# Layer 0's feed-forward: context up projections first, main tokens with 7 of 8 block products, gated products through DRAM, three down passes

## The chip, the cores and the metric

The kernel runs on one core of a Trainium2 chip, as one program in one launch. A core has a matrix engine (TensorE; PE in the profile, PEld its weight loads), VectorE (DVE), ScalarE (ACT), GpSimd (POOL) and SyncE (SP), which here only issues DMAs. The metric is the device time of one execution in microseconds (us); lower is better.

## The reference, cut to what matters

A two-layer transformer over 1024 main tokens and 256 context tokens of width 1024: layer 0 mixes with window and differential attention, layer 1 with gated linear attention (GLA). Each layer ends with a feed-forward of width 2816 with a convolution of 3 tokens. Layer 0 runs it on main and context tokens, layer 1 on main tokens alone. All values are float32.

```python
def conv_ffn(x, w_up, conv_w, conv_b, w_down):
    h = x @ w_up                       # [n, 1024] x [1024, 5632]
    h = lax.conv_general_dilated(h, ...) + conv_b      # each column: tokens t-1, t, t+1
    u, gt = jnp.split(h, 2, axis=-1)
    return (jax.nn.silu(gt) * u) @ w_down              # [n, 2816] x [2816, 1024]

for layer in range(2):
    ...
    h = h + g1 * y
    h = h + g2 * conv_ffn(rms_norm(h, norm2_g[layer]) * (1.0 + sc2) + sh2, ...)
    if need_ctx:                                       # layer 0
        hc = hc + cg1 * yc
        hc = hc + cg2 * conv_ffn(rms_norm(hc, norm2_g[layer]) * (1.0 + csc2) + csh2, ...)
```

## The kernel before

**Numbers.** Every operand of a large matmul is split into a high and a low part of a shorter float format (`split`, line 97: ACT casts the high part at L100, DVE subtracts to get the low part at L80). A product is three matmuls: high x high, high x low, low x high.

**Layout.** Features lie on the 128 partitions, tokens along the free axis. `h[k]` (k = 0 to 7) holds the residual stream, 1280 tokens: main blocks MAIN0 and MAIN1 of 512, then CTX of 256.

**Weights.** `load_w` (line 103) loads one block of 1024 x 128 weights (512 KB) with one DMA from SP into one of two raw buffers (`wraw`), and splits it in two halves of 512 columns into four of the twelve `wf` buffers (names `wh`, `wl`), so that the weights of three blocks can stand ready. A raw buffer is free again after DVE's second subtraction.

**Layer 0's feed-forward** (`ffn`, line 898) goes through 22 blocks c of 128 hidden features. For each, two up blocks (u and gate) are multiplied with all 1280 tokens into three PSUM banks (`big`, `proj` L130: 8 k x 3 matmuls for MAIN0, CTX and MAIN1), ACT and DVE apply the convolution (`cv`), ACT the silu, DVE the product, and the result is split into `gh`, `gl` in SBUF. After every second c, `down` (L923) multiplies the waiting pair with its two blocks of `ffn_down`, 8 output blocks d for each of CTX, MAIN0, MAIN1, and DVE adds each result to `h` (L77). The steps of layer 1's modulation (`mod_steps`: 32 blocks of 512 KB into `mraw`, two buffers, each reduced by DVE at L290) are laid between, two for each c. The norms ahead (`norm_mod`) and those of layer 1 behind (`norm3`) sum their squares first.

**Layer 1's feed-forward** is written in another way. `ffn_halves` (line 1060) splits the 1024 main tokens in two halves, the 1024 inputs in two halves, and pairs the u and gate blocks of a c; the 2 x 2 x 2 products of such blocks are made with seven products of sums and differences instead of eight (`forms_first`, `forms_last` build the token operands B11, B21, B22, T1 to T4 from `h`, whose memory then serves as workspace; `pair_forms` builds the weight operands). The gated products go to DRAM (`gs`, POOL's queue). `down_pass` (line 1157) runs once for each 512 tokens: eight PSUM banks collect over all 22 blocks, each with its weights loaded anew and its `gs` rows loaded into `dx` and split into `dh`, `dl`.

**What sets the order.** The Tile scheduler fixes the order of each engine's instructions when the program is built; engines run their lists in order and wait on semaphores. Inside `manual_schedule` PE's list follows the program text. In layer 0 that holds from the second half of the attention output to the first up blocks; in layer 1 from the output projection to the end. SP issues its DMAs in list order, and a DMA whose buffer is not free holds up those behind it.

## Time and profile before

| | us |
|---|---|
| median of 3 runs (3154.15 to 3158.14) | 3154.94 |
| the profiled execution | 3159.17 |
| its span, first to last instruction | 3157.4 |
| PE busy in it | 2999.3 (95%) |
| layer 0's feed-forward, start of its first up and of its last down matmul | 914.3 to 1864.0 |
| layer 1's feed-forward, start of its first block product and of its last down matmul | 2451.6 to 3140.4 |

A row of a view shows start and duration in us. A matmul's duration includes its flow through the array, so that neighbours overlap: what a matmul costs in a row of them is the distance between two starts. In a row of groups the first number after the bar is busy time, the second the mean of one instruction in ns. A bracket at the end of a row of the timeline is the time that the engine sat idle before it, and what ended that.

### The profile page before, as it was taken

The page shows a single profiled execution, that of the slowest core. Times are in us where ns is not written, and L with a number is a line of the kernel's source. Part 1 is how long each engine was busy: PE and PEld are TensorE (multiplying, and loading weights), DVE is VectorE, ACT ScalarE, POOL GpSimd, SP SyncE. Part 2 cuts the span into 40 slices and gives each one's busy share as a digit, 9 for nine tenths or more (in the row PEclk, how much of TensorE's full clock was granted, in tenths as well). Part 3 has the DMA queues.
Part 4 walks back from the last instruction along what each step waited for, and adds up shares of the span by engine and source line. Part 5 has one row for each costly group of instructions (what it writes and reads, how often), then busy time and mean ns, then how long its engine had stood idle before and what let it go on. Part 6 is the DMA issues. An engine that isn't in the chain of part 4 may idle for free.

```text
span 3157.4 us, 40797 instructions
## 1 busy us (share of the span) xinstructions
PE 2999.3 (95%) x16024; PEld 2523.0 (80%) x16024; DVE 2140.0 (68%) x3520; ACT 1290.8 (41%) x2301; POOL 50.5 (2%) x88
## 2 busy tenths in 40 slices
PE   8887789999999999999999999999999799999998
PEld 4676779998877888888888878888887588888886
DVE  7667578887478645555554498687686888887354
ACT  5111167777352222222222265454454444445332
POOL 0000000000000000000000000000001000000000
PEclk9988889999999999999999999999999999999999
DMA  6665582121525311111111132111134222225452
GB/s 218 180 177 164 154 203 67 55 61 34 174 81 164 110 34 41 41 34 41 35 38 36 38 131 74 51 36 42 51 112 157 66 88 80 81 80 166 151 169 95
DMA packets 154296, 300.50 MB, mean 95 GB/s; under 512 B 24468, under 2 KB 81940, under 8 KB 154104
## 3 DMA queue, kind: packets, MB, share of 16 engines
q1 hardware_dynamic: 133400, 261.94, 26.0%
q0 software_dynamic: 19552, 33.87, 3.8%
q8 instruction: 126, 2.06, 0.3%
q10 hardware_dynamic: 1152, 2.10, 0.2%
q14 instruction: 66, 0.54, 0.1%
HBM read 246.69 MB, written 51.12 MB: 94 GB/s over the span
## 4 chain that ended last, share of the span: by engine, by line
PE 77%; DVE 12%; DMA 6%; ACT 3%; issue 1%; SPq 0%; DVEq 0%; ACTq 0%
PE big L130 31%; PE bk L1090 13%; PE sm L923 9%; PE bk L1175 7%; DMA mraw<-in_mod_wt_dram 5%; PE sm L534 2%; PE sm L583 2%; PE sm L649 2%; PE big L509 2%; PE big L468 2%; PE sm L1610 2%; PE big L517 2%; DVE mraw L290 1%; PE sm L1541 1%; DVE junk L290 1%
## 5 line engine op out<-in xcount | busy, mean ns | idle before, releaser
L100 ACT CAST wh<-wraw 128x512 fp32r<-128x512 f32 x436 | 268.4, 621 | 897.8 <-PE big L130 444.6
L80 DVE TENSOR_TENSOR wl<-wraw,wh 128x512 fp32r<-128x512 f32 x436 | 299.6, 689 | 421.8 <-ACT wh L100 402.0
L130 PE MATMUL big<-x2h,wh 128*128 128x512 f32 (+1 forms) x1056 | 377.9, 358 | 2.4 <-ACT x2h L83 1.3
L130 PE MATMUL big<-x2l,wh 128*128 128x512 f32 (+1 forms) x1056 | 377.7, 358 | 0.4 <-DVE x2l L77 0.3
L130 PE MATMUL big<-x2h,wl 128*128 128x512 f32 (+1 forms) x1056 | 377.4, 357 | 0.0
L77 DVE SCALAR_TENSOR_TENSOR h<-sm,G,h 128x512 f32<-128x512 f32 (+1 forms) x280 | 180.8, 657 | 79.7 <-PE sm L923 78.8
L130 PEld LDWEIGHTS big<-x2h,wh 128*128 128x128 f32 x1056 | 199.1, 189 | 34.3 <-ACT crow L83 2.0
L130 PEld LDWEIGHTS big<-x2l,wh 128*128 128x128 f32 x1056 | 199.1, 189 | 32.5 <-DVE x2l L77 1.1
L130 PEld LDWEIGHTS big<-x2h,wl 128*128 128x128 f32 x1056 | 199.0, 188 | 30.4
L923 PE MATMUL sm<-gh,wh 128*128 128x512 f32 (+1 forms) x528 | 190.9, 361 | 6.3 <-DVE h L77 6.0
L923 PE MATMUL sm<-gl,wh 128*128 128x512 f32 (+1 forms) x528 | 188.6, 357 | 0.0
L923 PE MATMUL sm<-gh,wl 128*128 128x512 f32 (+1 forms) x528 | 187.9, 356 | 0.0
L77 DVE SCALAR_TENSOR_TENSOR cv<-big,cw,cv 128x255 f32<-128x255 f32 (+1 forms) x176 | 155.0, 881 | 31.8 <-ACT cv L83 29.6
L130 PE MATMUL big<-x1h,wh 128*128 128x512 f32 (+1 forms) x336 | 126.3, 379 | 33.8 <-DVE slo L80 32.7
L1175 PE MATMUL bk<-dh,wh 128*128 128x512 f32 x352 | 137.3, 390 | 0.0
L1175 PE MATMUL bk<-dl,wh 128*128 128x512 f32 x352 | 136.9, 389 | 0.0
L1175 PE MATMUL bk<-dh,wl 128*128 128x512 f32 x352 | 136.9, 389 | 0.0
L290 DVE CUSTOM_DVE_ANT_0 junk<-mraw,crow 128x1024 bf16<-128x1024 f32 x56 | 68.5, 1223 | 99.5 <-DMA mraw<-in_mod_wt_dram 99.5
L83 ACT ACTIVATE cv<-big,cb,cw 128x1024 f32<-128x1024 f32 x88 | 77.8, 884 | 135.7 <-DVE cv L77 134.5
L130 PE MATMUL big<-x1h,wl 128*128 128x512 f32 (+1 forms) x336 | 125.8, 375 | 3.9 <-DVE wl L80 3.9
L130 PE MATMUL big<-x1l,wh 128*128 128x512 f32 (+1 forms) x336 | 125.8, 375 | 0.0
L923 PEld LDWEIGHTS sm<-gh,wh 128*128 128x128 f32 x528 | 100.4, 190 | 29.6 <-DVE h L77 14.7
(442 smaller groups left out, 7491.0 us busy)
## 6 DMA issues: line engine op xcount, KB each, us to landing
mraw<-in_mod_wt_dram SPq DMA_DIRECT2D x88, 512.0 KB, 4.5
wraw<-in_ffn_up_dram SPq DMA_DIRECT2D x66, 512.0 KB, 3.7
wraw<-in_ffn_down_dram SPq DMA_DIRECT2D x66, 512.0 KB, 3.7
graw<-in_ffn_up_dram SPq DMA_DIRECT2D x22, 512.0 KB, 3.7
gs<-hh POOLq DMA_DIRECT2D x22, 512.0 KB, 2.9
dx<-gs SPq DMA_DIRECT2D x44, 256.0 KB, 3.8
q<-qs SPq DMA_DIRECT2D x40, 256.0 KB, 3.3
q<-qs SPq DMA_DIRECT2D x80, 128.0 KB, 3.5
```

What stands on the lines that cost most here:

```text
L77: return self.nc.vector.scalar_tensor_tensor(out=out, in0=in0, scalar=scalar, in1=in1, op0=op0, op1=op1)
L80: return self.nc.vector.tensor_tensor(out=out, in0=a, in1=b, op=op)
L83: return self.nc.scalar.activation(out=out, in_=in_, func=func, **kw)
L100: self.nc.scalar.copy(hi, src)
L130: self.nc.tensor.matmul(ps[:, t0:t0 + n], self.columns(a, k * m, m), b(k, t0, n), start=(k == 0 and j == 0), stop=(k == KD - 1 and j == 2))
L290: self.nc.vector.tensor_tensor_reduce(out=out, in0=raw, in1=row, scale=1.0, scalar=0.0, op0=ALU.mult, op1=ALU.add, accum_out=dst[:, v:v + 1])
L468: self.nc.tensor.matmul(ps[:, 256 * b:256 * b + 256], a(k, t0, P), self.columns(w, k % 4 * 256, 256), start=(k == 0 and j == 0), stop=(k = ...
L509: nc.tensor.matmul(out, q[:, 0, s, :], key, start=True, stop=False)
L517: nc.tensor.matmul(out, q[:, 1, s, :], key, start=False, stop=True)
L923: nc.tensor.matmul(o, self.columns(w, d * P, P), x[:, t0:t0 + n], start=(i == 0), stop=(i == 3 * len(group) - 1))
L1090: nc.tensor.matmul(ps, a[:, s], b, start=(start and k == 0 and j == 0), stop=(k == 3 and j == 2), skip_group_check=True)
L1175: nc.tensor.matmul(ps[d], self.columns(a, d * P, P), b, start=(c == 0 and j == 0), stop=(c == NFF - 1 and j == 2))
```

## The change

Layer 0's feed-forward takes the form of layer 1's, with the context on a path of its own.

- `h` becomes main tiles `hm` of 1024 tokens and context tiles `hc` of 256.
- `out_pass` sums the squares of what it writes (`sums`), and writes the new main rows of `h` to DRAM (`h2`). The norm's mean is one matmul with the sum (`mean`). The same in layer 1.
- `ffn_ctx`: the 44 up blocks for the 256 context tokens alone, the products to DRAM (`gx`). Twelve of the twenty steps of `forms_last` are laid between its blocks c = 1 to 12.
- `ffn_halves` for the main tokens (44 up blocks loaded again), products to `gs`.
- three `down_pass`es, for MAIN0, CTX and MAIN1, each loading the 22 blocks of `ffn_down`. The first has the 32 modulation blocks and the reload of `h` from `h2` between its blocks, the second `norm3` of MAIN0 and the gate weights of GLA, the third `norm3` of CTX.
- PSUM goes to eight single banks ahead of `ffn_ctx`, and back to two `big` and two `sm` buffers after the third pass. PE follows the program text from the attention output to the end of the third pass.

```diff
-    def ffn(self, l, fp, xh, xl, h, NT, first, in_order, last_norm, step, before_last, after_last, after):
...
+    def conv(self, y, x, j):
+
+        cw, n = self.cw[:, j, :], y.shape[1]
+        self.act(y, x, AF.Identity, scale=cw[:, 1:2], bias=self.cb[:, j:j + 1])
+        self.stt(y[:, 1:], x[:, :n - 1], cw[:, 0:1], y[:, 1:], ALU.mult, ALU.add)
+        self.stt(y[:, :n - 1], x[:, 1:], cw[:, 2:3], y[:, :n - 1], ALU.mult, ALU.add)
+
+    def ffn_ctx(self, l, fc, xh, xl, step):
+
         for c in range(NFF):
             cv = []
             for part in range(2):
                 j = c + NFF * part
...
+                self.urgent = True
+                w = self.load_w(self.io["ffn_up"][l, j])
+                self.urgent = False
+                ps = self.bank()[:, :NX]
+                self.proj(ps, w, lambda k, a, b: xh[k], lambda k, a, b: xl[k], ((0, NX),))
+                y = fc.tile([P, NX], F32, name=f"cx{part}", tag=f"cx{part}", bufs=2)
+                with self.tc.high_priority():
+                    self.conv(y, ps, j)
                 cv.append(y)
...
+            self.last = self.act(cv[1], cv[1], AF.Silu)
             self.tt(cv[0], cv[0], cv[1], ALU.mult)
...
+            self.dma2(self.gx[c], cv[0])
             step(c)
...
+    def mean(self, acc, ps=None):
+
+        n = acc.shape[1]
+        ps = self.sm() if ps is None else ps
+        self.nc.tensor.matmul(ps[:, :n], self.onesm, acc, start=True, stop=True)
+        return ps
...
-    def down_pass(self, l, h, t0, dp, mid={}, after=None, begin=None):
+    def down_pass(self, l, h, t0, n, dp, mid={}, after=None, begin=None):
...
-            self.dma(x, self.gs[c][:, t0:t0 + 512])
...
+            self.dma(x, self.gx[c] if v else self.gs[c][:, t0:t0 + n])
...
+        def step(c):
+            if c == 0:
+                todo.append(self.forms_last(hm, X, A[:, :, 0], B[:, :, 0], self.mean(acc)))
+            if 0 < c <= 12:
+                next(todo[0])
+        self.ffn_ctx(0, fc, ch, cl, step)
...
+        self.ffn_halves(0, fw, hm, X, lambda: None, lambda ps: list(todo[0]))
...
+        def rows(i, k):
+            self.dma(hm[k][:, 512 * i:512 * i + 512], self.h2[k][i])
+
+        def steps(c):
+            if 2 <= c < 2 + 2 * KD:
+                rows((c - 2) // KD, (c - 2) % KD)
             for _ in range(2):
                 next(st["mod"], None)
...
+        self.down_pass(0, h, 0, 512, dp, {c: lambda c=c: steps(c) for c in range(1, NFF)}, squares(0))
...
+        begin, mid = lag(0, 512)
+        mid[1] = begin
+        mid[12] = gate_weights
+        self.down_pass(0, h, NM, NX, dp, mid, squares(NM))
+        begin, mid = lag(NM, NX)
+        self.down_pass(0, h, 512, 512, dp, mid, squares(512), begin)
+        in_order.close()
+        self.es_ps.close()
+        self.open_psum()
```

**PE, in the feed-forward of layer 0.** Before, where one up block ends (512 columns of MAIN1) and a down product begins with CTX:

```order
L130 MATMUL big<-x2h_8069,wh 128x512
L130 MATMUL big<-x2l_8077,wh 128x512
L130 MATMUL big<-x2h_8069,wl 128x512
L923 MATMUL sm<-gh,wh 128x256
L923 MATMUL sm<-gl,wh 128x256
L923 MATMUL sm<-gh,wl 128x256
```

After, where the last context up block ends and the first block product of the main tokens begins (x2ch, x2cl: the context tokens' two parts; B11: main tokens 0 to 511, inputs 0 to 511):

```order
L140 MATMUL bk<-x2ch_7604,wh 128x256
L140 MATMUL bk<-x2cl_7612,wh 128x256
L140 MATMUL bk<-x2ch_7604,wl 128x256
L1052 MATMUL bk<-B11h_8186,wh 128x512
L1052 MATMUL bk<-B11l_8187,wh 128x512
L1052 MATMUL bk<-B11h_8186,wl 128x512
```

The context's 256 columns stood with 1024 main columns on the same weights; now each loaded block meets 256 columns alone, 24 matmuls. In the whole lists layer 0's feed-forward goes from 3168 up matmuls (2112 of 512 columns) and 1584 down ones (1056 of 512) to 1056 of the context's up blocks (256 columns), 1848 block products (512), and again 1584 down ones.

**DVE, between two convolutions.** Before, in the steady part (`wl`: weights' low halves; `cv`: convolution; `h`: results of `down`):

```order
L80 TENSOR_TENSOR wl<-wraw,wh 128x512 x3
L77 SCALAR_TENSOR_TENSOR cv_11459<-big,cw,cv_11459 128x1023 x2
L77 SCALAR_TENSOR_TENSOR cv_11459<-big,cw,cv_11459 128x255 x2
L80 TENSOR_TENSOR cv_11161<-cv_11161,cv_11459 128x1280
L80 TENSOR_TENSOR gl<-cv_11161,gh 128x1280
L80 TENSOR_TENSOR wl<-wraw,wh 128x512 x2
```

After, in the context up projections (`cx0`, `cx1`: convolution of u and gate), around a step of `forms_last` (B22):

```order
L90 TENSOR_TENSOR wl_9368<-wraw_9365,wh_9367 128x512
L87 SCALAR_TENSOR_TENSOR cx1_9316<-bk_9291,cw_8637,cx1_9316 128x255
L90 TENSOR_TENSOR wl_9372<-wraw_9365,wh_9371 128x512
L87 SCALAR_TENSOR_TENSOR B22l1_8625<-h5_7567,B01_88,B22h1_8624 128x512
L90 TENSOR_TENSOR wl_9413<-wraw_9410,wh_9412 128x512
L87 SCALAR_TENSOR_TENSOR cx0_9361<-bk_9336,cw_8637,cx0_9361 128x255
L90 TENSOR_TENSOR wl_9417<-wraw_9410,wh_9416 128x512
```

The two splits of each weight block were followed by work on 1280 tokens; now they alternate with convolutions of 256 tokens, and the steps of the forms stand in the same list.

**SP's queue, at the modulation blocks.** Before, at the start of layer 0's feed-forward:

```order
L86 DMA wraw<-in_ffn_up_dram 128x1024 x4
L86 DMA wraw<-in_ffn_down_dram 128x1024
L86 DMA mraw<-in_mod_wt_dram 128x1024 x2
L86 DMA wraw<-in_ffn_up_dram 128x1024 x2
L86 DMA mraw<-in_mod_wt_dram 128x1024 x6
```

After, in the first down pass (`dx`: gated products from DRAM; `h`: rows of the residual stream from `h2`):

```order
L96 DMA dx<-gs_165 128x512
L96 DMA h_7564<-h_120 128x512
L96 DMA mraw<-in_mod_wt_dram 128x1024
L96 DMA wraw<-in_ffn_down_dram 128x1024
L96 DMA mraw<-in_mod_wt_dram 128x1024 x2
L96 DMA dx<-gs_166 128x512
L96 DMA h_7565<-h_122 128x512
```

The modulation blocks stand two to each block of the down pass; the weights for its block c = 18 stand behind the last of the 32.

## Rows read from the trace of the kernel before

**Rows 1.** The page: span, and busy time of PE, with its share.

```profile
span 3157.4 us, 40797 instructions
PE 2999.3 (95%) x16024; PEld 2523.0 (80%) x16024; DVE 2140.0 (68%) x3520; ACT 1290.8 (41%) x2301; POOL 50.5 (2%) x88
```

**Rows 2.** The page: the chain that ended last, by engine.

```profile
PE 77%; DVE 12%; DMA 6%; ACT 3%; issue 1%; SPq 0%; DVEq 0%; ACTq 0%
```

**Rows 3.** One line's or tile's instructions, PE: durations, first and last start in us.

```profile
L130 PE MATMUL big<-x2h,wh x1056: 278/392/795, 914.3 to 1809.8; 128*128 128x512 f32 x131, 128*128 128x256 f32 x45
L923 PE MATMUL sm<-gh,wl x528: 278/389/419, 977.7 to 1864.0; 128*128 128x512 f32 x110, 128*128 128x256 f32 x66
```

**Rows 4.** Timeline of ACT, layer 0: cast of the gated products, c and c+2.

```profile
1372.73 1.27 ACT L100 CAST gh<-cv 128x1280 fp32r<-128x1280 f32 x1 [1.56 <-DVE cv L80]
1456.44 1.27 ACT L100 CAST gh<-cv 128x1280 fp32r<-128x1280 f32 x1 [1.56 <-DVE cv L80]
```

**Rows 5.** Timeline of POOL, layer 1: gated products to DRAM, c and c+1.

```profile
2563.37 0.53 POOL L90 DMA_DIRECT2D gs<-hh  x1 [18.69 <-DVE hh L80]
2582.59 0.53 POOL L90 DMA_DIRECT2D gs<-hh  x1 [18.69 <-DVE hh L80]
```

**Rows 6.** Timeline of SP's queue, layer 1's first down pass: weight loads, c and c+1.

```profile
2923.50 0.33 SPq L86 DMA_DIRECT2D wraw<-in_ffn_down_dram  x1
2928.94 0.33 SPq L86 DMA_DIRECT2D wraw<-in_ffn_down_dram  x1
```

**Rows 7.** Timeline of PE, GLA's context: first of 24 matmuls of 256 columns, and the next.

```profile
1867.08 0.28 PE L130 MATMUL big<-x3ch,wh 128*128 128x256 f32 x1
1869.89 0.28 PE L1498 MATMUL sm<-rstc,w2s 128*128 128x256 f32 x1
```

**Rows 8.** Timeline of SP's queue, GLA's context: three weight loads in a row.

```profile
1888.20 0.33 SPq L86 DMA_DIRECT2D wraw<-in_gla_w_qk_dram  x1
1891.35 0.33 SPq L86 DMA_DIRECT2D wraw<-in_gla_w_v_dram  x1
...
1894.45 0.33 SPq L86 DMA_DIRECT2D wraw<-in_gla_w_v_dram  x1
```

**Rows 9.** Groups of DVE's instructions by form, 900 to 1900 us.

```profile
L80 DVE TENSOR_TENSOR wl<-wraw,wh 128x512 fp32r<-128x512 f32 x154 | 106.2, 690 | 222.8 <-ACT wh L100 215.3 <-PE sm L923 6.5
L77 DVE SCALAR_TENSOR_TENSOR cv<-big,cw,cv 128x255 f32<-128x255 f32 x88 | 42.3, 481 | 18.3 <-ACT cv L83 17.1
L290 DVE CUSTOM_DVE_ANT_0 mraw<-mraw,crow 128x1024 f32<-128x1024 f32 x32 | 39.1, 1223 | 17.6 <-DMA mraw<-in_mod_wt_dram 17.3
L77 DVE SCALAR_TENSOR_TENSOR nu<-h,A,yr 128x512 f32<-128x512 f32 x16 | 11.3, 745 | 0.0
```

**Rows 10.** Busy by window: length, PE, PEld, DVE, ACT, POOL, granted clock, DMA share, GB/s.

```profile
400.00:440.00 40.00, 31.91 (x198) 27.44 (x197) 28.22 (x89) 22.62 (x85) 0.00 (x0) 0.80 1.16 271
1200.00:1400.00 200.00, 200.00 (x1042) 170.47 (x1041) 104.92 (x141) 44.54 (x55) 0.00 (x0) 1.00 0.11 36
1870.00:1890.00 20.00, 17.56 (x143) 16.70 (x141) 19.58 (x41) 17.37 (x44) 0.00 (x0) 1.00 0.39 116
2413.00:2420.00 7.00, 5.95 (x12) 4.08 (x13) 2.69 (x5) 2.38 (x4) 0.00 (x0) 0.51 0.29 94
2452.00:2520.00 68.00, 52.10 (x189) 36.52 (x188) 61.76 (x91) 34.72 (x53) 0.79 (x2) 0.90 0.18 59
```

**Rows 11.** Timeline of PE: waits at a norm's mean, and at layer 1's first block product.

```profile
902.93 0.67 PE L148 MATMUL sm<-acc,onesm 128*128 128x256 f32 x2 [2.38 <-DVE acc L80]
2414.05 1.19 PE L148 MATMUL sm<-acc,onesm 128*128 128x512 f32 x1 [4.12 <-DVE acc L80]
2451.56 0.47 PE L1090 MATMUL bk<-B11h,wh 128*128 128x512 f32 x1 [0.94 <-DVE hh L77]
```

**Rows 12.** Timeline of SP's queue, layer 0: six modulation blocks in a row.

```profile
966.75 14.83 SPq L86 DMA_DIRECT2D mraw<-in_mod_wt_dram  x6
```

**Rows 13.** Layer 1's down passes, loads of `dx`: time from issue to landing.

```profile
DMA to landing us min/median/max: 3.1/3.8/6.2
```

More of the change, by code (lines that the diff above doesn't have):

```diff
@@ L32, with __init__, __getitem__ @@
 LAM_INIT = 0.8 - 0.6 * math.exp(-0.3 * 0)
+class Rows:
+    def __init__(self, m, c):
+        self.m, self.c = m, c
+    def __getitem__(self, key):
+        p, s = key
+        return self.m[p, s] if s.start < NM else self.c[p, s.start - NM:s.stop - NM]
 class K:
@@ L961, in ffn @@
-                cv.append(y)
-                if full and (part or 7 < c < NFF - 1):
-                    if c < NFF - 1:
-                        down(load(full), order)
-                    else:
-                        late = load(full)
-                        down(late, order[:-1], urgent=True)
-                    full = []
-            last = self.act(cv[1], cv[1], AF.Silu)
-            self.tt(cv[0], cv[0], cv[1], ALU.mult)
-            gh = fp.tile([P, NT], F32R, name="gh", tag="gh", bufs=gb)
@@ L972, in ffn @@
-            gl = fp.tile([P, NT], F32R, name="gl", tag="gl", bufs=gb)
-            self.split(gh, gl, cv[0])
-            group.append((c, gh, gl))
-            if c % 2 == 0:
-                full, group = group, []
-            step(c)
-        self.exp_tables(last)
-        before_last()
-        group = load(group)
-        after_last()
-        down(group, order[:-1], after, True)
-        down(late + group, ((512, 256), (768, 256)) if NT == NM else order[-1:], after, True)
-        for t in lag:
-            after(*t)
+                self.urgent = True
@@ L1135, in ffn_halves @@
         prod(q, 2)
-        ps = self.bank()
-        nc.tensor.matmul(ps, self.onesm, acc, start=True, stop=True)
+        ps = mean()
         nxt = begin(1)
@@ new lines, in body @@
+        self.ffn_ctx(0, fc, ch, cl, step)
+        es_f.close()
+        es_c.close()
+        self.close_tmp()
+        X |= self.forms(self.pool(es_x, "xn2d", side="right"), ("T3", "T4"))
+        fw = self.pool(es_f, "ffw")
+        self.ffn_halves(0, fw, hm, X, lambda: None, lambda ps: list(todo[0]))
+        self.exp_tables(self.last)
+        es_f.close()
+        es_x.close()
+        es_q = self.stack()
+        qp = self.pool(es_q, "sumsq")
+        acc = qp.tile([P, 512], F32, name="sumsq")
@@ L1304, in after_last, with squares @@
-        def after_last():
+        def squares(t0):
+            n = accs[t0].shape[1]
+            return lambda d: self.add_square(accs[t0], h[d][:, t0:t0 + n], d)
+        st["mod"] = self.mod_steps([(1, j) for j in range(2, 6)], self.mod_rows(mp, 1), mp)
+        self.down_pass(0, h, 0, 512, dp, {c: lambda c=c: steps(c) for c in range(1, NFF)}, squares(0))
+        for _ in st["mod"]:
+            pass
+        self.close_tmp()
+        es_m.close()
+        st["es0"], st["esw"], st["es"], st["es2"] = (self.stack() for _ in range(4))
@@ L1336, in after, with norm3 @@
-        def after(t0, n):
-            if (t0, n) == MAIN1:
-                es_f.close()
-                self.urgent = True
-                self.gla_ctx(st)
-            norm3(t0, n)
-        self.ffn(0, fp, xh, xl, h, T, first, in_order, last_norm, step, before_last, after_last, after)
+        A, B = self.A[1][0], self.B[1][0]
+        def norm3(t0, n, ps=None):
+            ps = self.mean(accs[t0], ps)
+            with self.tc.high_priority():
+                y = self.rstd_of(ps, n)
+            yield
+            for k in range(KD):
+                if t0 == NM:
+                    self.norm_chunk(k, lambda k, a, b: hc[k], st["ch"], st["cl"], 0, n, A[:, :, 1], B[:, :, 1], y)
+                else:
+                    self.norm_chunk(k, lambda k, a, b: hm[k][:, a:a + b], st["h"], st["l"], t0, n, A[:, :, 0], B[:, :, 0], y)
+                yield
@@ new lines, in lag, with begin @@
+        def lag(t0, n):
+            def begin(ps=None):
+                todo.append(norm3(t0, n, ps))
+                next(todo[-1])
+            return begin, {c: lambda: next(todo[-1], None) for c in range(2, 2 + KD)}
+        begin, mid = lag(0, 512)
[5 more added lines that the diff above has]
+        in_order.close()
@@ L1343, in body @@
+        self.es_ps.close()
+        self.open_psum()
+        es_f.close()
+        norm = norm3(512, 512)
+        self.urgent = True
+        self.gla_ctx(st)
+        for _ in norm:
+            pass
+        self.urgent = False
         self.close_tmp()
         st["es2"].close()
+        es_q.close()
         for k in range(KD):
-            self.dma(self.hs[k], h[k][:, :NM])
+            self.dma(self.hs[k], hm[k])
         es_h.close()
```

245 lines of the change are left out of this document (95 added, 150 removed).

## The prediction

> **What bounds the kernel now.** The page comes first: PE is busy for 95% of the span [rows 1], and the chain that ended last runs through PE for 77% of it [rows 2]. The stretch that is rewritten runs from 914.3 to 1864.0 us [rows 3]; with the last matmul's 0.2 us that is 949.9 us. Inside it a window of 200 us holds 200.00 us of PE at full clock [rows 10], with DVE at 52% and the DMA engines at 11%. So matmuls set the time of layer 0's feed-forward, and everything else has room. What to watch is whether that stays so when the same matmuls are spread over more loads.
>
> Steady costs, each as the distance between two rows that repeat:
> - Layer 0 before: the gated products of c and c+2 are cast 83.71 us apart [rows 4], so one c costs 41.85 us and 22 cost 920.7. The other 29.2 us of the stretch are norm means, the modulation's start, the waits at the first blocks and slow clock after them.
> - Block products as layer 1 has them: 19.22 us for one c [rows 5].
> - A down pass of 512 tokens as layer 1 has it: 5.44 us for a block [rows 6].
> - 256 columns: 24 matmuls take 2.81 us [rows 7].
>
> **What the change does to PE.** 264 of 2112 up matmuls of 512 columns disappear. Priced with the steady costs: block products 22 x 19.22 = 422.8; two main down passes 2 x 22 x 5.44 = 239.4; context up 44 x 2.81 = 123.6; context down 22 x 2.81 = 61.8. The sum is 847.6 us against 920.7. That is the gain if nothing but PE sets the time: 73 us.
>
> **What the context's own loads cost.** A loaded block of 512 KB now feeds PE for 2.81 us. In the trace, three loads in a row with only two raw buffers start 6.25 us apart, first to third [rows 8]: landing, cast, two subtractions, then the buffer is free. No triple need be the closest that can be, so I take a little over it, 6.33: 3.17 us for a load. The twelve `wf` buffers give three blocks of stock, which is used up within some ten loads.
> - Context up, c = 1 to 12: DVE has four subtractions of 0.690, four convolution steps of 0.481, a product near 0.48 [rows 9], 5.2 us, and one step of the forms. A step is two or three operations at 0.69 to 0.745 [rows 9], 1.6 us in the mean. 6.8 us in all; DVE has been 98% full where it set the pace [rows 10], so about 7.0 us for each c where PE needs 5.62. 12 x 7.0 = 84.0.
> - The other ten c go at the pace of the raw buffers: 10 x 6.33 = 63.3. Context up then takes 147.3 us, 23.7 over PE's 123.6.
> - Context down: 22 x 3.17 = 69.7; in eight of them `norm3` adds two operations of 0.745 [rows 9] to DVE, some 2 us in all; GLA's three small weight loads pass through the same two raw buffers, at most three turns (9.5 us), at least nothing; I take 5. 76.7 us, 14.9 over PE.
>
> The floor of both excesses is zero (the stock hides them), the ceiling about twice my values (every buffer turn near 8 us under mixed DMA traffic).
>
> **The other new costs in the stretch.**
> - Start of the block products. Layer 1's start spends 68.0 us on 189 matmuls [rows 10], which at 19.22/84 = 0.229 us are 43.3: 24.7 lost, partly to forms that were not ready. Here twelve of twenty form steps are done during the context and the first halves of the rest too. Between 0 and 24.7 I take 5, nearer to the low end, because one wait remains by construction: for c = 0 and 1, product 4 follows product 7 in the same bank, which DVE must read in between.
> - First down pass. The modulation's 32 blocks move from the up loop into 22 blocks of 5.44 us. Alone on the queue they go 2.90 us apart (14.83 less one issue of 0.33, over five) [rows 12]. Beside other loads a landing takes up to 6.2 us [rows 13]; with DVE's 1.223 [rows 9] and two buffers that is 3.7 us apart. The load for c = 18 stands behind the last of them on SP, and PE wants it 18 x 5.44 = 98 us after the pass began. The queue reaches the first modulation block about 6 us before the pass begins, and a weight block is usable about 6 us after its issue, so it comes at 32 x r: 93 us for r = 2.9 (hidden), 119 for 3.7 (21 late). With r between them at 3.3: 106, 8 us late.
> - The norm means, the modulation's start and the change of PSUM layout: 4; handing over from pass to pass, with stocks that run dry at each tail: 2. Slow clock in the context stretches: 3, see the third rival.
>
> New stretch: 422.8 + 239.4 + 147.3 + 76.7 + 5 + 8 + 4 + 2 + 3 = 908.2 us, 41.7 less than 949.9. GLA's first loads no longer start under the last down matmuls, since PE's list is now fixed to the end of the third pass: 2 (0 to 8). The change back to `big` waits for the last eviction, like the 0.94 us at layer 1's change [rows 11]: 1.
>
> **What goes away elsewhere.** The wait of 2.38 us at the context's norm [rows 11] is hidden, since the sums of squares are ready a pass earlier. In layer 1 the mean waits 4.12 us for its sum [rows 11], and the following 7 us run at a granted clock of 0.51 [rows 10], another 3.4 us; the mean now follows a full block of the next pass, so about 7 of these 7.5 go. Behind it, layer 1's first block product is the next late thing, and it is unchanged.
>
> Sum: -41.7 + 2 + 1 - 2.4 - 7 = -48.1 us. The profiled execution has 3159.2 us, so 3111; it lies 4.2 above the median of the runs, so the forecast is **3107 us**.
>
> **The edits that cost nothing.** Squares summed in `out_pass` (ACT and DVE): PE works 5.4 us or more on each block there, DVE's share grows to about 3 us. The 16 rows to `h2`, the `gx` and `gs` writes: POOL is busy for 2% and only issues [rows 1]; the cover is gone only if DMA were full, which counts in the first down pass alone. Twenty-two `gx` rows back through SP: small, inside the pace of the raw buffers.
>
> **Rivals.**
> 1. *The loads starve more than I count*: modulation blocks at r = 3.7 (21 us late instead of 8) and a third more excess in both context passes (13 us). 3107 + 26 = 3133, with 3124 to 3148 around it. For it: GLA's context loads needed 6.25 us for two in one of their closest triples [rows 8], on a DVE that was 98% full [rows 10]. Against: the stock of three blocks.
> 2. *The excess is hidden*: both context passes at PE's pace, no late block in the first pass. 3107 - 23.7 - 14.9 - 8 = 3060, up to 3090. Against: a buffer turn of 6.25 us has no row below it, and two blocks need only 5.62 us of PE.
> 3. *The clock falls in the context stretches, and the kernel becomes slower.* Rows show a granted clock of 0.80 in a window where PE was 80% busy with gaps throughout, and 1.00 where it was 88% busy [rows 10]. My context stretches have PE 80 to 84% busy at full clock. At the lower level (1.2 GHz) their 185.4 us of matmuls become 370.8, 147 more than the 224 they have in the forecast: 3254. It decides when 185.4 / clock exceeds 224 + 48, below a mean granted clock of 0.68. Against: at half clock PE is busy all the time, so the gaps that led there are gone and the clock would return, as it did after each dip.
>
> The Trainium skill, "TensorE: Matmul & The Clock Gate", section "HAM oscillation — how this bites in real kernels", describes just this: compute for each weight tile shorter than the wait for the next, and the engine throttled again at every tile. By it the time would be rival 3's. The row with 88% busy at full clock does not bear that out for short gaps.
>
> That the change would not do what it says is excluded: the built lists hold 1848 block products in place of 2112 matmuls.
>
> **How the numbers follow.** Forecast, 3092 to 3124: 0.60. Rival 1: 0.20. Rival 2: 0.09. Rival 3: 0.05. Between rival 1 and no gain (3148 to 3161): 0.06. The range from 3084 to 3142 holds the forecast, most of rival 1 and the upper edge of rival 2: 0.8. A measurement tells 0.2% (6 us) from no change: faster by more (below 3148.6) 0.91, within it 0.04, slower 0.05.
>
> **What would show it.** Context up: a new c every 7.0 us, then 6.3, PE 80 to 90% busy, DVE near full. Block products: 19.2 us for each c from the third on. First down pass: 5.44 us between weight loads is right only if the modulation is hidden; a hole of about 8 us near its end shows the step right. Context down: 3.2 us for a block. Layer 1: no wait at its mean. It would be wrong if a step of block products took over 19.5 us, if the granted clock stood at half for long, or if the second feed-forward moved.

## The result, and the profile after

The changed kernel takes 3119.6 us (median of 4 runs, 3117.4 to 3123.0) against 3156.5 for the kernel before on the same chips: ratio 0.988, 95% interval 0.9865 to 0.9899. It is faster by 1.2%, 37 us between the medians where 48 were forecast; 3119.6 lies inside the range and 12.6 us above the forecast of 3107. The profiled execution took 3117.4 us, 41.7 less than the 3159.2 of before; the forecast for it was 3111. It was the shortest of its four, and the one of before lay above its median, so the miss is 6.4 us there.

The page, answering to [rows 1, 2]: PE's busy time fell by 64 us, and its share of the chain from 77% to 69%, with 7% "issue" that was 1%.

```profile
span 3115.7 us, 41831 instructions
PE 2935.4 (94%) x15746; PEld 2474.1 (79%) x15746; DVE 2275.7 (73%) x3805; ACT 1476.9 (47%) x2690; POOL 82.7 (3%) x148
...
PE 69%; DVE 11%; DMA 8%; issue 7%; ACT 3%; POOL 1%; SPq 0%; DVEq 0%; ACTq 0%; POOLq 0%
```

Timeline of PE, the first matmuls of stages and the longest waits (answering to [rows 3, 11]):

```profile
909.59 0.36 PE L140 MATMUL bk<-x2ch,wh 128*128 128x256 f32 x1 [0.94 <-DVE h L87]
...
1050.76 0.39 PE L1052 MATMUL bk<-B11h,wh 128*128 128x512 f32 x1
...
1055.39 0.50 PE L1052 MATMUL bk<-B21h,wh 128*128 128x512 f32 x1 [1.67 <-ACT p L1060]
...
1487.71 1.88 PE L295 MATMUL bk<-crow,onesm 128*128 128x512 f32 x4
1491.54 0.61 PE L1137 MATMUL bk<-dh,wh 128*128 128x512 f32 x1 [1.95 <-ACT dh L110]
...
1620.83 0.28 PE L1137 MATMUL bk<-dh,wh 128*128 128x256 f32 x1
...
1668.18 0.58 PE L1137 MATMUL bk<-dh,wh 128*128 128x256 f32 x1 [7.58 <-ACT wh L110]
...
1690.95 0.38 PE L1137 MATMUL bk<-dh,wh 128*128 128x256 f32 x1 [2.74 <-ACT wh L110]
...
1708.00 0.40 PE L1137 MATMUL bk<-dh,wh 128*128 128x512 f32 x1
...
1829.55 0.32 PE L140 MATMUL big<-x3ch,gwhi 128*48 128x256 f32 x1 [1.20 <-DVE h L87]
...
2409.76 0.47 PE L1052 MATMUL bk<-B11h,wh 128*128 128x512 f32 x1 [0.94 <-DVE hh L87]
```

Read as stages, from the first matmul of one to the first of the next:

| stage | forecast | measured |
|---|---|---|
| context up | 147.3 | 141.2 |
| block products | 422.8 + 5 | 436.9 |
| row of the modulation (in "means": 4), first down pass (119.7 + 8) | 131.7 | 133.1 |
| context down | 76.7 | 87.2 |
| third pass, to GLA's first matmul (119.7 + 2 + 1) | 122.7 | 121.6 |
| handovers and slow clock, counted apart | 5 | in the stages |
| sum; before: 949.9 | 911.2 | 920.0 |
| ahead of it (before to 914.3, after to 909.6) | -2.4 | -4.7 |
| GLA and its output, to layer 1's first product (before 587.4) | -7 | -7.1 |
| the rest (before 705.8) | 0 | +0.1 |

Timeline of POOL, which issues each finished gated product (answering to [rows 4, 5]): context products of c = 6 to 8 and of c = 10 to 12, main products of layer 0, main products of layer 1.

```profile
958.62 0.54 POOL L100 DMA_DIRECT2D gx<-cx  x1 [5.46 <-DVE cx L90]
964.61 0.54 POOL L100 DMA_DIRECT2D gx<-cx  x1 [5.45 <-DVE cx L90]
970.46 0.54 POOL L100 DMA_DIRECT2D gx<-cx  x1 [5.31 <-DVE cx L90]
...
985.08 0.54 POOL L100 DMA_DIRECT2D gx<-cx  x1 [6.67 <-DVE cx L90]
992.17 0.54 POOL L100 DMA_DIRECT2D gx<-cx  x1 [6.55 <-DVE cx L90]
999.31 0.54 POOL L100 DMA_DIRECT2D gx<-cx  x1 [6.60 <-DVE cx L90]
...
1204.07 0.53 POOL L100 DMA_DIRECT2D gs<-h  x1 [18.99 <-DVE h L90]
1223.59 0.54 POOL L100 DMA_DIRECT2D gs<-h  x1 [18.99 <-DVE h L90]
...
2560.39 0.53 POOL L100 DMA_DIRECT2D gs<-hh  x1 [18.70 <-DVE hh L90]
2579.62 0.53 POOL L100 DMA_DIRECT2D gs<-hh  x1 [18.69 <-DVE hh L90]
```

The context takes 5.9 us for a c early and 7.1 for c = 9 to 13 (counted at the issue of the products; PE works about two c ahead of it). And the same 84 matmuls take 19.52 us in layer 0 and 19.23 in layer 1, in one execution.

Busy by window (columns as in [rows 10]): context up early and at c = 9 to 13, block products, first down pass before and in its waits, the hole in the context's pass and that pass's end.

```profile
915.90:940.00 24.10, 24.10 (x200) 23.86 (x199) 22.79 (x45) 17.44 (x33) 2.16 (x4) 1.00 0.53 172
975.00:1012.00 37.00, 32.45 (x243) 29.88 (x242) 30.38 (x59) 21.80 (x43) 3.23 (x6) 1.00 0.57 173
1200.00:1400.00 200.00, 200.00 (x862) 162.13 (x861) 163.81 (x215) 94.55 (x133) 5.85 (x11) 1.00 0.24 82
1500.00:1567.00 67.00, 66.31 (x293) 54.58 (x291) 45.50 (x76) 17.96 (x30) 0.00 (x0) 1.00 0.85 290
1567.00:1574.00 7.00, 5.43 (x16) 4.07 (x17) 5.30 (x10) 2.38 (x4) 0.00 (x0) 0.76 1.02 380
1660.00:1672.00 12.00, 4.42 (x21) 3.99 (x21) 4.21 (x8) 3.92 (x7) 0.42 (x1) 0.74 0.56 159
1690.00:1700.00 10.00, 6.41 (x24) 5.18 (x24) 5.21 (x10) 3.63 (x7) 0.00 (x0) 0.66 0.50 175
```

The granted clock is 1.00 through context up, though PE is 88% busy at c = 9 to 13. In layer 0's feed-forward it falls at four places: at the start of the first down pass, behind two waits of 1.68 and 0.58 at 1568, at the hole of 7.58 and at the end of that pass; behind the wait of 1.67 at 1055 it stays at 1.00.

### The profile page after: what moved, and what is told of

The parts are those of the page before. It is cut to its first block, busy times and chain, and to the rows that moved or that the text cites. A ratio compares the mean times of both kernels' runs of the same rounds, so it can differ in the third digit from the quotient of the medians.

```text
span 3115.7 us, 41831 instructions
## 1 busy us (share of the span) xinstructions
PE 2935.4 (94%) x15746; PEld 2474.1 (79%) x15746; DVE 2275.7 (73%) x3805; ACT 1476.9 (47%) x2690; POOL 82.7 (3%) x148
## 4 chain that ended last, share of the span: by engine, by line
PE 69%; DVE 11%; DMA 8%; issue 7%; ACT 3%; POOL 1%; SPq 0%; DVEq 0%; ACTq 0%; POOLq 0%
PE bk L1052 26%; PE bk L1137 14%; PE big L140 12%; DMA mraw<-in_mod_wt_dram 5%; PE sm L552 2%; PE big L486 2%; PE sm L601 2%; PE sm L667 2%; PE big L527 2%; PE sm L1626 2%; PE big L535 2%; DVE mraw L308 1%; PE sm L1557 1%; DMA wraw<-in_ffn_down_dram 1%; DVE junk L308 1%
## 5 line engine op out<-in xcount | busy, mean ns | idle before, releaser
L1137 PE MATMUL bk<-dh,wh 128*128 128x512 f32 (+1 forms) x880 | 329.5, 374 | 18.5 <-ACT wh L110 11.8
L1137 PE MATMUL bk<-dl,wh 128*128 128x512 f32 (+1 forms) x880 | 327.9, 373 | 2.5 <-DVE dl L90 2.5
L1137 PE MATMUL bk<-dh,wl 128*128 128x512 f32 (+1 forms) x880 | 327.5, 372 | 0.2 <-DVE wl L90 0.2
L110 ACT CAST wh<-S 128x512 fp32r<-128x512 f32 x176 | 108.8, 621 | 225.9 <-DVE S L90 116.7
L1137 PEld LDWEIGHTS bk<-dh,wh 128*128 128x128 f32 x880 | 168.6, 192 | 49.9 <-ACT wh L110 12.4
L1137 PEld LDWEIGHTS bk<-dl,wh 128*128 128x128 f32 x880 | 168.9, 192 | 32.4 <-DVE dl L90 4.2
L1137 PEld LDWEIGHTS bk<-dh,wl 128*128 128x128 f32 x880 | 168.7, 192 | 28.8 <-DVE wl L90 0.9
L90 DVE TENSOR_TENSOR wl<-S,wh 128x512 fp32r<-128x512 f32 x176 | 120.5, 686 | 11.3 <-ACT wh L110 11.2
L87 DVE SCALAR_TENSOR_TENSOR h<-h,cw,h 128x1023 f32<-128x1023 f32 x88 | 111.0, 1280 | 16.4 <-ACT h L93 16.3
L87 DVE SCALAR_TENSOR_TENSOR hh<-hh,cw,hh 128x1023 f32<-128x1023 f32 x88 | 111.1, 1280 | 14.7 <-ACT hh L93 14.7
```

Of the source, the lines that this page charges most:

```text
L87: return self.nc.vector.scalar_tensor_tensor(out=out, in0=in0, scalar=scalar, in1=in1, op0=op0, op1=op1)
L90: return self.nc.vector.tensor_tensor(out=out, in0=a, in1=b, op=op)
L110: self.nc.scalar.copy(hi, src)
L1137: nc.tensor.matmul(out(d), self.columns(a, d * P, P), b, start=(c == 0 and j == 0 and d % per == 0), stop=(c == NFF - 1 and j == 2), skip_ ...
```

## The experiments

All twelve against the changed kernel, by stage (us; "c" is one c of block products). The first 860 us, up to the attention output's second half, took 861.4 to 868.8 in the executions that leave them unchanged. So an effect of a few us is read from its stage, not from the whole time.

| kernel | median | ratio to before, 95% | context up | c in layer 0, 1 | first pass | context down | GLA output |
|---|---|---|---|---|---|---|---|
| changed | 3119.6 | 0.9865-0.9899 | 141.2 | 19.52, 19.23 | 129.3 | 87.2 | 111.6 |
| e1 offsets | 3115.7 | 0.9848-0.9885 | 142.6 | 19.04, 19.60 | 128.5 | 88.9 | 111.6 |
| e2 gate weights | 3115.4 | 0.9856-0.9885 | 141.0 | 19.60, 19.23 | 126.5 | 84.8 | 111.9 |
| e3 modulation | 3119.4 | 0.9863-0.9897 | 140.6 | 19.60, 19.23 | 126.7 | 88.4 | 111.7 |
| e4 three buffers | 3099.0 | 0.9802-0.9833 | 132.1 | 19.52, 19.23 | 126.0 | 79.3 | 113.5 |
| e5 left shifted | 3117.5 | 0.9865-0.9895 | 141.3 | 19.04, 19.60 | 130.5 | 87.4 | 112.3 |
| e6 old mean | 3132.6 | 0.9916-0.9952 | 141.7 | 19.60, 19.23 | 129.8 | 87.8 | 123.1 |
| e7 = e2 + e4 | 3088.4 | 0.9773-0.9808 | 132.1 | 19.52, 19.23 | 126.3 | 69.7 | 113.4 |
| e8 crow | 3120.8 | 0.9876-0.9905 | 140.9 | 19.52, 19.23 | 128.5 | 88.9 | 111.9 |
| e9 = e7 + pads | 3078.2 | 0.9740-0.9767 | 130.6 | 19.04, 19.04 | 128.4 | 69.9 | 113.3 |
| e10 | 3078.8 | 0.9737-0.9769 | 131.2 | 19.04, 19.04 | 129.4 | 69.1 | 113.9 |
| e11 | 3074.4 | 0.9728-0.9755 | 130.8 | 19.04, 19.04 | 126.2 | 68.9 | 113.4 |
| e12 four steps | 3118.9 | 0.9855-0.9895 | 136.8 | 19.52, 19.23 | 127.9 | 86.0 | 112.0 |

**e1: why is a c dearer in layer 0?** The tiles' addresses are in the built program; the pad moves the operands of the block products and, of all else, only the norm's row that lies beside them.

```diff
         es_x = self.stack()
+        self.pool(es_x, "pad0", side="right").tile([P, 32], F32, name="pad0")
         X = self.forms(self.pool(es_x, "xn2", side="right"), ("B11", "B21"))
...
         es_x = self.stack()
+        self.pool(es_x, "pad1", side="right").tile([P, 48], F32, name="pad1")
         X = self.forms(self.pool(es_x, "xn4", side="right"), ("B11", "B21"))
```

> The changed kernel with one unused tile ahead of the token operands of each layer's block products: 128 bytes in layer 0, 192 in layer 1. In the built program the operands of layer 0 then begin at 96 modulo 256 bytes instead of 224, those of layer 1 at 224 instead of 160; nothing else moves. In the changed kernel one c of block products takes 19.52 us in layer 0 and 19.23 in layer 1, though both are 84 matmuls of 512 columns; the down passes, whose operands begin at 96, take 226.7 ns for a matmul. Theory: the place in SBUF sets the slot. Layer 0 goes to 84 x 0.2267 = 19.04 us for each c (-0.48 x 22 = -10.6), layer 1 to 19.52 (+0.29 x 22 = +6.4), whole time -4. Rival: it is what runs beside PE in layer 0 (DVE, DMA): both stay as they are, whole time unchanged.

Timeline of POOL in e1, layer 0 and layer 1:

```profile
1201.62 0.53 POOL L100 DMA_DIRECT2D gs<-h  x1 [18.50 <-DVE h L90]
1220.66 0.53 POOL L100 DMA_DIRECT2D gs<-h  x1 [18.51 <-DVE h L90]
...
2612.02 0.53 POOL L100 DMA_DIRECT2D gs<-hh  x1 [19.07 <-DVE hh L90]
2631.62 0.53 POOL L100 DMA_DIRECT2D gs<-hh  x1 [19.07 <-DVE hh L90]
```

19.04 and 19.60: the place decides, and the layers trade places. (At a distance of 128 bytes a c takes 19.52 in some executions and 19.60 in others, as the table shows for layer 0.) The block products of layer 0 took 426.6 us (before the pad 436.9), those of layer 1 456.7 (449.2). What runs beside them did not change, so the rival falls.

**e5: which place?** The pad stands ahead of the weights, on the left, and leaves the block products' operands where they were.

```diff
         self.wp = self.pool(es, "w")
+        self.wp.tile([P, 32], F32, name="padw")
```

> The changed kernel with an unused tile of 128 bytes ahead of the weight buffers. In the built program it shifts every tile on the left of SBUF by 128 bytes: the weights' halves, the down passes' dh and dl, the context's x2ch go from 96 to 224 modulo 256; the operands of the block products, on the right, stay at 224 (layer 0) and 160 (layer 1). Which place counts? Theory A, the distance between moving operand and weights: layer 0's block products, now at distance 0, fall from 19.52 to 19.04 us for a c, the down passes stay at 226.7 ns a matmul, layer 1's products change (distance 64 the other way round). Theory B, the moving operand's own place, 96 being the good one: layer 0's products stay at 19.52, the down passes, now at 224, rise from 5.44 to 5.58 us a block (24 x 232.4 ns), layer 1 stays at 19.23. Whole time: A about -10, B about +12 (88 blocks of 512 at +0.14).

Timelines of e5: POOL in both layers, and SP's weight loads in the third pass.

```profile
1200.39 0.53 POOL L100 DMA_DIRECT2D gs<-h  x1 [18.51 <-DVE h L90]
1219.43 0.53 POOL L100 DMA_DIRECT2D gs<-h  x1 [18.51 <-DVE h L90]
...
2614.00 0.53 POOL L100 DMA_DIRECT2D gs<-hh  x1 [19.07 <-DVE hh L90]
2633.60 0.53 POOL L100 DMA_DIRECT2D gs<-hh  x1 [19.07 <-DVE hh L90]
```

```profile
1744.06 0.33 SPq L96 DMA_DIRECT2D wraw<-in_ffn_down_dram  x1
1749.50 0.33 SPq L96 DMA_DIRECT2D wraw<-in_ffn_down_dram  x1
```

Theory A holds at all three places: layer 0 at 19.04 with its operands untouched, the down passes still at 5.44 after moving together with the weights, layer 1 slower, by 7.8 us for its stage, so that the whole time falls by 2 us where about 10 were expected. What counts is the distance between moving operand and weights.

**e2: the gate weights moved to the third pass.**

```diff
-        mid[12] = gate_weights
         self.down_pass(0, h, NM, NX, dp, mid, squares(NM))
         begin, mid = lag(NM, NX)
+        mid[12] = gate_weights
```

> The changed kernel with GLA's gate weights loaded in the third down pass (its block 12) instead of the context's pass (its block 12). Theory: the three small loads, with eleven DMAs on SP, hold both raw buffers, so that PE waits 7.58 us for the next weight block at 1668 us and then runs at a low granted clock. Moved behind blocks of 5.44 us they cost nothing: the context's pass goes from 87.2 us to 75 to 77, the third pass stays at 121.5, whole time -11. Rival: the hole is the norm's work on DVE or the queue, which remain: the context's pass stays above 84, or the hole of 7 us turns up in the third pass; whole time within 3 us.

SP's queue in the changed kernel shows the cause; for 8.6 us it issues no weight block:

```profile
1655.11 0.33 SPq L96 DMA_DIRECT2D wraw<-in_gla_gate_w_dram  x1
...
1659.14 1.27 SPq L96 DMA_DIRECT2D wraw<-in_gla_gate_w_dram  x3
1660.46 0.59 SPq L96 DMA_DIRECT2D wraw<-in_gla_gate_b_dram  x2
1661.16 1.24 SPq L96 DMA_DIRECT2D wraw<-in_gla_gate_w_dram  x3
1662.44 0.57 SPq L96 DMA_DIRECT2D wraw<-in_gla_gate_b_dram  x2
1663.71 0.36 SPq L96 DMA_DIRECT2D wraw<-in_ffn_down_dram  x1
```

PE in e2, and the window at the end of its context pass:

```profile
1663.22 0.38 PE L1137 MATMUL bk<-dh,wh 128*128 128x256 f32 x1 [1.09 <-ACT wh L110]
...
1693.47 0.58 PE L1137 MATMUL bk<-dh,wh 128*128 128x256 f32 x1 [3.51 <-ACT wh L110]
```

```profile
1690.00:1700.00 10.00, 5.52 (x21) 4.71 (x21) 4.10 (x9) 1.97 (x4) 0.00 (x0) 0.54 0.57 199
```

The hole is gone, and the third pass stays at 121.6; but the pass gained 2.4 us, not 11. So the rival's number came, above 84, but not its reason: the hole went with the gate weights. Behind it the next limit was waiting: PE now waits for weights at many blocks from the eleventh on, and longest at the last three, which must all be loaded before the first output; the clock falls there instead.

**e4 and e7: three raw buffers, alone and with e2.** Ten halves of split weights instead of twelve, since no more fits beside the other pools.

```diff
-        return self.wp.tile([P, 1024], F32, name="wraw", tag="wraw", bufs=2)
+        return self.wp.tile([P, 1024], F32, name="wraw", tag="wraw", bufs=3)
...
-        hi, lo = (self.wp.tile([P, 512], F32R, name=n, tag="wf", bufs=12) for n in ("wh", "wl"))
+        hi, lo = (self.wp.tile([P, 512], F32R, name=n, tag="wf", bufs=10) for n in ("wh", "wl"))
```

> The changed kernel with three raw weight buffers instead of two for the whole program, and ten halves of split weights (2.5 blocks in stock) instead of twelve, so that it fits. Context up takes 141.2 us, c = 9 to 14 at 7.1 us each. Theory of the prediction: after the stock is used up the turn of two raw buffers sets the pace, so a third one brings context up near PE's own 1056 x 0.120 = 126.7: 127 to 131, and the context's pass from 87.2 to about 80 (the gate weights still stand in its way); whole time -12 to -20. Rival 1: DVE is the limit while the forms are built: c = 9 to 14 stay at 7.0 or more, context up 138 or more. Rival 2: the smaller stock costs as much as the third buffer gives, here or in other stages: whole time unchanged or slower.

> The gate weights in the third pass and three raw buffers (ten halves in stock) together. Alone the first left the context's down pass at 84.8 us, the second at 79.3, of 63.8 that PE needs at 2.88 a block and 0.45 for the mean. Theory: with the gate weights away, the turn of two raw buffers had become the limit, and with three buffers, the gate weights; both together bring the pass to 70 to 74, the rest being the tail, where the last three blocks must all be loaded before the first output. Context up 132 as with three buffers alone. Whole time 5 to 8 below three buffers alone (3099). Rival: DVE's norm work or the tail is the limit: the pass stays at 78 or more.

The window of e4 at the same time as that of c = 9 to 13:

```profile
975.00:1012.00 37.00, 36.34 (x291) 35.03 (x290) 33.13 (x66) 24.48 (x48) 3.17 (x6) 1.00 0.61 191
```

PE is 98% busy where it was 88%, while DVE does more, 33.1 us instead of 30.4. So DVE had not been the limit; the turn of two buffers had, as the prediction's other term said. Context up fell to 132.1 (PE's floor is 1056 x 0.120 = 126.7), context down to 79.3; with the gate weights away as well, to 69.7 (floor 63.8). The gate weights are worth 2.4 us with two buffers and 9.6 with three: each was hidden behind the other. The place is the pass's end: its last three blocks take 11.7 us more than their steady 8.6 in the changed kernel, 13.4 in e2 and 11.2 in e4, but 4.9 in e7, where the only waits over 0.3 us are those for DVE's evictions. e7's whole time lies 10.6 us below e4's, where 5 to 8 were expected. The block products (439.3) and GLA's output (113.5) grew by some 2 us each; that the smaller stock does this was not tested apart.

**e12: four of the forms' steps in context up instead of twelve.**

```diff
-            if 0 < c <= 12:
+            if 0 < c <= 4:
                 next(todo[0])
```

> The changed kernel with four of the twelve steps of the block products' operands left between the context's up projections (c = 1 to 4) and eight moved behind them, to the other eight ahead of the fifth block product. Prediction's step: each of the steps adds to DVE's 5.2 us for a c and so to the context's pace (7.0 instead of 6.3). Theory: c = 9 to 14 fall from 7.1 to about 6.3, as two raw buffers allow: context up 141.2 to 136 to 138; the eight steps come back ahead of the block products, whose stage (437 us, 7.5 over its steady 429.4) grows by 8 to 15; whole time +3 to +10. Rival: the pace is the buffers' alone: context up stays within 1 us of 141.

The window of e12 at that time:

```profile
975.00:1012.00 37.00, 35.28 (x279) 33.85 (x278) 32.81 (x65) 23.62 (x45) 3.24 (x6) 1.00 0.58 179
```

Context up 136.8, as the theory said, with PE 95% busy there: the steps do lengthen the turn, because they stand in DVE's list between the subtractions that set a raw buffer free. The second half was wrong: the eight steps behind it cost nothing (block products 436.7 us against 436.9). Their place in the context was a loss of 4.4 us. In the whole time, where +3 to +10 was expected, it can't be told from the scatter.

**e3: one modulation block instead of two for each block of the first pass**, the rest in the third.

```diff
-            x = dp.tile([P, 512], F32, name="dx", tag="dx", bufs=4)[:, :n]
+            x = dp.tile([P, 512], F32, name="dx", tag="dx", bufs=2 if l == 0 else 4)[:, :n]
...
-            for _ in range(2):
-                next(st["mod"], None)
+            next(st["mod"], None)
...
+        mid = {c: lambda c=c, f=mid.get(c): (f and f(), next(st["mod"], None)) for c in range(2, NFF - 3)}
         self.down_pass(0, h, 512, 512, dp, mid, squares(512), begin)
```

> The changed kernel with one modulation block to each block of the first down pass instead of two, and the rest (about 14) one to a block in the third pass; to make room, two dx buffers instead of four in layer 0's passes. The first pass takes 129.3 us where 22 x 5.44 = 119.7. Theory: 5.7 of the 9.6 us over are blocks that wait at c = 12 to 18 because 512 KB weights, two modulation blocks, gated products and rows of h together are more than the DMA engines bring in 5.44 us; halved they are hidden: first pass 123.5, third pass 121.5 to 123, whole time -5. Rival: they are DVE's or SP's queue, or two dx buffers starve the passes in their turn: first pass 128 or more, third pass longer, whole time 0 to +8.

The third pass hides its share (121.5). The waits at c = 13 to 18 are gone, but one of 1.8 us at the end with a slow clock behind it takes their place; whether the two `dx` buffers bring it was not tested. First pass 126.7: that is inside what kernels with all 32 blocks in it show (126.0 to 130.5). Inconclusive on the 5.7 us.

**e8: the modulation's row from DRAM instead of PE and ACT.**

```diff
+            self.crow_d = self.dp.tile([P, 1024], F32, name="crow_d")
+            self.dma2(self.crow_d, rows[0])
...
-        st["mod"] = self.mod_steps([(1, j) for j in range(2, 6)], self.mod_rows(mp, 1), mp)
+        crow = mp.tile([P, 1024], F32, name="crow0")
+        self.dma(crow, self.crow_d)
+        st["mod"] = self.mod_steps([(1, j) for j in range(2, 6)], [crow], mp)
```

> The changed kernel with the row of the conditioning vector that the modulation blocks are multiplied with (crow) taken over from the start of the program through DRAM (one write there, one load here of 512 KB) instead of being built again by eight ACT copies, two matmuls and two evictions ahead of the first down pass. There PE waits: 3.83 us from the end of the block products to the first down matmul, then 1.95, then a low clock for some 7 us. Theory: the way over PE and ACT makes the hole; without it the first down matmul follows the last product within 1 us and the first block takes 5.5 instead of 9.3: whole time -5 to -7. Rival: the hole is the first gated products' way through DRAM and their split: it stays at 3 us or more, and whole time within 2 us.

PE in e8, and SP's queue at the same place in the changed kernel:

```profile
1493.86 0.50 PE L1139 MATMUL bk<-dh,wh 128*128 128x512 f32 x1 [3.06 <-ACT dh L110]
1496.18 0.79 PE L1139 MATMUL bk<-dl,wh 128*128 128x512 f32 x1 [1.83 <-DVE dl L90]
```

```profile
1481.62 1.03 SPq L96 DMA_DIRECT2D mraw<-in_mod_wt_dram  x2
1483.47 0.33 SPq L96 DMA_DIRECT2D wraw<-in_ffn_down_dram  x1
1483.85 1.87 SPq L96 DMA_DIRECT2D dx<-gs  x4
```

The rival holds: the hole stays, since the gated products stand behind two modulation blocks and the weights (behind a third such load in e8) and land 6 to 7 us after their issue. The row lay beside that wait, and was not its cause.

**e6: layer 1's first mean as before.**

```diff
-        self.out_pass(io["gla_w_out"], ((MAIN0, oA),), h, self.G[1][0], first, sums={0: acc0})
+        self.out_pass(io["gla_w_out"], ((MAIN0, oA),), h, self.G[1][0], first)
...
+        def norm_first():
+            for k in range(KD):
+                self.add_square(acc0, h[k][:, :512], k)
+            self.forms_first(h, X, A, B, self.mean(acc0))
...
```

> The changed kernel with layer 1's first norm mean as the kernel before has it: the squares of MAIN0 are summed after the second output block of the next pass, instead of in the pass that writes MAIN0. From the start of GLA's output projection of the second tokens to the first block product the changed kernel has no wait over 0.6 us before the first product. Theory: the mean's wait of 4.1 us and the slow clock behind it come back, output projection 111.6 to 119, whole time +7. Rival: the 7 us came from elsewhere in GLA (its start, its shorter list): the stage stays at 111.6 and whole time within 2 us.

PE and the window behind it:

```profile
2388.02 2.05 PE L185 MATMUL sm<-sumsq,onesm 128*128 128x512 f32 x2 [8.23 <-DVE sumsq L90]
```

```profile
2387.00:2396.00 9.00, 7.98 (x22) 5.77 (x23) 4.03 (x7) 3.11 (x5) 0.00 (x0) 0.65 0.00 0
```

The wait and the slow clock return. They cost 11.4 us, more than the 7.3 that this stage (GLA's output: 118.9 before, 111.6 after) had gained, since the sum comes even later here than in the kernel before (a wait of 8.2 instead of 4.1).

**e9 to e11: together.** e9 is e7 with pads of 128 and 64 bytes where e1 has its pads; e10 moves the context's operands by 64 bytes (a pad ahead of x2ch, an offset within dh and dl); e11 has pads at the right end for all large products.

```diff
-            xh = dp.tile([P, 512], F32R, name="dh", tag="dh", bufs=4)[:, :n]
...
+            xh = dp.tile([P, 512], F32R, name="dh", tag="dh", bufs=4)[:, 16 * v:16 * v + n]
...
+        cp.tile([P, 16], F32, name="padc")
...
```

> Gate weights in the third pass, three raw buffers (ten halves), and a pad of 128 bytes (layer 0) and 64 bytes (layer 1) ahead of the operands of the block products, so that both layers' operands begin at the same place modulo 256 as the weights (96). The parts have been measured apart: without the pads 3088 us. Theory, that the distance between moving operand and weights sets the slot: 19.04 us for a c in both layers, -0.48 x 22 and -0.19 x 22, together -14.7: 3073. Rival, that the parts share what they save: not under 3080.

> The one before it (e9) with the operands of the context's 256-column matmuls moved 64 bytes up: x2ch, x2cl and, in the context's down pass, dh and dl begin at 160 modulo 256, the weights at 96. In the traces 256-column matmuls at distance 0 take 120.0 ns each (x2ch), those at 64 114 to 117 (GLA's x3ch). Theory: with 256 columns a distance of 64 is better than none: with three raw buffers PE is the limit in context up, so 132 goes to 127 to 129, the context's pass from 69.7 to about 68, whole time -3 to -6. Rival: 114 to 117 belongs to GLA's other surroundings, or the loads are at their limit already: within 1 us.

> e10 with the pads at the right end of SBUF instead (128 bytes from the start, 192 more in GLA, 192 more ahead of GLA's context operands), so that also the operands of the first projections (x1h), of the attention output (oA, 233 ns a matmul now), of GLA's projections (x3h) and of its output (gA, 229 ns) come to the place of the weights. Theory: about 650 x 6 ns in the first projections, 192 x 6 in the attention output, some 500 x 2.4 in GLA, less some 3 ns on their 256-column parts: -4 to -7. Rival: the shift changes the attention's small matmuls for the worse by as much: 0 to +5.

e9: a c takes 19.04 us in both layers, their stages fall by 10.0 and 3.0 us, against 14.7 expected; the whole comes to 3078, between the theory's 3073 and the rival's 3080. e10: 256-column matmuls go from 120.0 to 117.6 ns, not to 114, and the stages hold still, as the rival said; that the loads are nearly their limit was not tested: a miss in time. e11: matmuls of 512 columns go from 232.8 to 228.1 ns in the first projections, from 232.9 to 229.1 in the attention output; its whole time, 3074.4, can't be told from e10's. Its median is the lowest here, 0.974 of the kernel before and about 45 us under the changed one.

## Why the prediction was right, and where its steps were not

Direction and range held because PE's sum held: 64 us of its busy time went where 73 were counted, and the context's loads took a part back, as forecast. That the sum missed by so little is in part luck: block products, context down and first pass came 21 us dearer than their terms, and context up, the third pass and the 5 us counted for handovers and slow clock gave 12 of them back. Step by step, on the profiled execution (6.4 us above the forecast for it):

- **Steady cost of block products: mis-sized, 6.6 us.** 19.22 came from layer 1 [rows 5] and was taken as the price of 84 matmuls; it was their price at that layer's addresses. At layer 0's it was 19.52 (e1, e5), just over the 19.5 that the prediction named as a sign of being wrong. In the same way 2.81 for 24 matmuls of 256 columns [rows 7] became 24 x 0.120 = 2.88. A price taken from another stage carries that stage's layout.
- **Start of the block products: 7.5 instead of 5**, by short waits for ACT and DVE evictions such as that of 1.67 at 1055.
- **Context up: 141.2 instead of 147.3.** The pace of 7.0 was right, for c = 9 to 13; up to c = 8 PE ran at its own pace, so that the stock covered more than the ten loads that were counted. Nor was a turn of 6.25 us the least of two buffers: five of those loads start within 12.2 us (from 945.4), a turn of 6.1. The reason given for 7.0, a full DVE, was wrong: in that window DVE was busy for 30.4 of 37 us, e4 removed the wait with more work on DVE, and e12 showed the steps' part in it, as work within the buffers' turn.
- **Context down: the step that failed, 87.2 instead of 76.7.** Priced were 3.17 us for each of 22 blocks, 2 for the norm and, between nothing and 9.5, 5 for the gate weights. In the trace PE takes 2.88 for most blocks and loses most of its time at two places. The gate weights are eleven DMAs that keep SP from issuing weight blocks for 8.6 us; PE stood for 7.58, and with the lower clock behind it two blocks took 10 us too long. At the pass's end the last three blocks took 20.3 us where 8.6 is steady: waits of 2.74 and 1.47 for weights, four of 0.6 to 0.9 for DVE's evictions, and a clock of 0.66. The prediction had 2 us for the tails of all passes together. And the terms don't add up as they were added: without the gate weights (e2) the pass still took 84.8, where the two other terms give 71.7. So the gate weights cost 2.4 us beside two raw buffers, not 5; what the sum lacked is the tail.
- **First pass: 133.1 with the row, 131.7 forecast**, but by other parts. The start cost more (3.8 for the row, then 1.95 and a slow first block), the waits at c = 13 to 18 took 5.7 us instead of 8 at c = 18, and they were for the split of the gated products (`dh`, `dl`), not for weights behind the modulation blocks. What the start waits for are the gated products (e8).
- **Layer 1's mean: -7.3 in its stage, -7 forecast**, and e6 brings it back. Of the -4.7 ahead of the stretch, 3.3 lie in the first 860 us, within their scatter; the attention output's second half gave 1.4 where 2.4 were forecast, and a wait of 0.94 is left ahead of the first up matmul. GLA's start and the PSUM change: 1.9 instead of 3.

The rivals: the first was true of context down alone, and there by the tail rather than by the pace of the loads. The second fell: with two buffers the excess was not hidden. The third fell clearly: context up kept a granted clock of 1.00 with PE 88 to 100% busy, and context down lost it only at the hole and at its end. The Trainium skill, "TensorE: Matmul & The Clock Gate", section "HAM oscillation — how this bites in real kernels", describes a kernel that is throttled at every tile because the compute of a tile is shorter than the wait for the next. The prediction put rival 3 under it, but that was not this case: 2.88 us of matmuls for each load stood against waits of about 0.5 and 0.2 us for a c of two loads, and the clock stayed. The waits that brought it down here were single ones, from 1.68 and 0.58 together up to 7.58 us.

## What to carry to other kernels

When matmuls are spread over more loads, count the turn of a load's buffers from issue to issue, with everything that stands in the subtracting engine's list between, count the small DMAs that pass the same buffers and queue by their number, and price the end of a pass, where several blocks must stand ready at once. A hole that is taken away shows only what the next limit leaves: two remedies worth 2.4 and 8 us alone were worth 17.5 together. And a duration from another stage is a price only if operands lie there as they will lie here.

## What the runs showed of the hardware that was not expected

A matmul of 512 columns in a full stream took 226.7 ns where moving operand and weights begin at the same place modulo 256 bytes, 228.9 at a distance of 64 bytes, 232.4 to 233.3 at 128 and 192 (distances of the starting addresses in the built program; block products of the changed kernel, e1 and e5, means of 850 to 880 matmuls each, from start to start). The down passes and the second half of both output projections, which lie at distance 0, took 226.7 to 227.2 in these three kernels. For 256 columns the order was another: 120.0 at distance 0, 117.6 at 64. The Trainium skill, "TensorE: Matmul & The Clock Gate", section "Step-by-step: what each phase is for", gives PE two independent read ports, one for the moving operand and one for the weights; that alone would not lead one to expect that the distance matters, and here it does, by up to 3%. Why was not found: no run here separates the weights' own load from the stream.
